# Products with the conditioning sums one turn later, and both context tiles behind the last token tile

## The chip, the cores and the metric

The kernel runs on one core of a Trainium2 chip. The metric is the device time of one execution in microseconds, the median of several runs.

## What is computed

One layer of a diffusion backbone over 1024 latent tokens of width 1024 and 256 context tokens. The part of the reference that matters here, cut:

```python
mod   = silu(c)     @ w_ada + b_ada          # 6 * 1024 numbers: shift, scale, gate, twice
mod_c = silu(c_ctx) @ w_ada + b_ada
h_lat = rms_norm(x, g_pre_mix)   * (1 + sc_m)  + sh_m
h_ctx = rms_norm(ctx, g_pre_mix) * (1 + csc_m) + csh_m
p_lat = h_lat @ w_in                         # 512 Fourier, 256 q, 128 kv, 32 rotary columns
p_ctx_kv = h_ctx @ w_in[:, KV_COL:]          # only kv and rotary columns
...
q = rms_norm(q_a, g_q_a) @ w_q_b             # later: attention, Fourier mixer, output projection
x = x + gt_m * rms_norm(y_lat, g_post_mix)
h2 = rms_norm(x, g_pre_ffn) * (1 + sc_f) + sh_f
x = x + gt_f * rms_norm(swiglu(h2), g_post_ffn)
```

All inputs are float32, and the result is wanted close to float32: every large product is made of three products of a "high" and a "low" half (`mm3`, or written out as in `back`).

## The kernel before

The kernel is cut into stages: the input projection (0 to about 150 us of the span), the Fourier mixer and the first query and key products, attention, the output projection, gate and up products of the channel mixer, and the down product. The change is in the second half of the input projection, `other_tiles` (from line 296), and at the start of `fourier`.

Eight token tiles of 128 rows (0 to 7) and two context tiles (c0, c1) are projected. Tiles 0 and 1 are done while `w_in` comes in (`first_tiles`). The other eight go through the loop of `other_tiles`, one turn each, in the order 2 to 7, c0, c1. For a tile there are these steps:

- `normed` (line 205): SyncE loads 128 rows to `xs`; ScalarE sums their squares (L86, `junk`); VectorE adds the epsilon (`var`), GpSimd takes the power (`rstd`) and scales the rows (L207).
- `transposed` (L212): TensorE turns the rows into a PSUM bank (`xT`).
- `front`: ScalarE applies shift and scale (L326, eight instructions, `h`), and makes the high half (`hh`, L50); VectorE makes the low half (`hl`, L56).
- `back` (L350): TensorE multiplies with `w_in`, 48 products for a token tile, 24 shorter ones for a context tile, into a bank `acc`.
- `after_project`: ScalarE copies the right columns of `acc` to `R` (L359, L362). For a token tile `fold` (L395 to L403) takes the Fourier columns on VectorE: tiles 0 to 3 are kept in `U`, with tiles 4 to 7 sums and differences are made (`eof`), which ScalarE and GpSimd split into halves (`Oh`, `Ol`, `EPh`, `EMh` and so on). Two buffers serve `eof`. Then `R` is normalized (GpSimd, L364 and L368) and its rotary columns are rotated (VectorE, `k1`, `k2`). The bank `acc` is free when the copy to `R` and the last reading by `fold` are done.
- `turn` (L382 to L388), a turn later: TensorE turns `R` into a bank `rps`, and ScalarE copies that to `q32`, `kv32`, `kr32`.

Beside this, two generators give out a few steps in each turn. `late_ada` makes three more parts of the conditioning: 24 blocks of `w_ada` of 512 KB are loaded into two buffers (`adraw`), and VectorE adds each, times its number, to a sum of 128 x 1024 (`adacc`, then `Gm`; L427, L429). After eight such sums a product with ones on TensorE (`gps`, L438 and L458) adds the partitions up; for the first two parts VectorE picks the diagonal (L440, `gdiag`) and reduces it (L442). `fourier_tables` loads the six slices of the transform's tables into two buffers (`traw`; L480); ScalarE makes their high halves (`toh`, `teh`) and GpSimd their low ones (`tol`, `tel`).

PSUM has eight banks of 2 KB a partition. `bankA` gives out three pieces of two banks in turn, to `xT`, `acc` and `gps`; `bankB` two pieces of one bank, to `rps`.

At the start of `fourier`, `attention_weights` loads the query, key and value weights; ScalarE scales them (`weight`, L588). The first transform (`positions(0)`, the products `po`, `pm`, `pp`) stands behind the last scaling of the query weights by `issue_after`, and then the rows of the last context tile are turned (`last_turn`), and the query products `qps` follow.

Each engine runs its instructions in order. The order is made when the program is built: the code's own order is the base, and a list scheduler of the framework moves instructions within an engine, so that a moved piece of code moves others too.

## Time and profile before

| | |
|---|---|
| median of 3 runs | 1269.03 us |
| lowest and highest run | 1265.46 and 1277.5 us |
| the profiled execution's own time | 1272.12 us |
| its span, first to last instruction | 1270.3 us |
| TensorE (PE) busy | 96% of the span |
| VectorE (DVE), ScalarE (ACT), GpSimd (POOL) busy | 69%, 50%, 40% |

The profile is one execution, read by an instruction timeline of each engine. A time in it is counted from the first instruction. A row that ends in brackets says how long the engine had stood idle before it and what the profile takes for the releaser; where that releaser had long been done, it was another one. POOL's spans are rough.

### The profile page before, as it was taken

What the parts mean: (1) busy time and instruction counts of PE and PEld (TensorE: products, weight loads), DVE (VectorE), ACT (ScalarE), POOL (GpSimd) and SP (SyncE); (2) the same over time, 40 slices, a digit from 0 to 9 for tenths busy, and PEclk for the clock granted to TensorE, in tenths of its full rate; (3) what the DMA queues carried; (4) which work ended last, traced back from release to release, by engine and by line L of the source; (5) the groups of instructions that cost most, each with busy time, mean ns of one, the idle gap of its engine ahead of it and who ended that gap; (6) DMA issues with size and microseconds to landing.
All of it is one profiled execution on the core that took longest, in us unless ns stands there. A gap on an engine that the chain in (4) does not pass through costs nothing.

```text
span 1270.3 us, 15471 instructions
## 1 busy us (share of the span) xinstructions
PE 1222.1 (96%) x5492; PEld 954.6 (75%) x5492; DVE 879.7 (69%) x1280; ACT 640.3 (50%) x1061; POOL 506.9 (40%) x332
## 2 busy tenths in 40 slices
PE   7999898999999998899999999999999999999997
PEld 5887676666666665678778888888888887887885
DVE  6777685555553546333778888777778775899697
ACT  6865657666767668265834444443344433222223
POOL 1275535777767770343183332233321300000083
PEclk8999989999999999899999999999999999999999
DMA  9576400000000015552025555342454368988645
GB/s 334 210 221 215 135 34 34 1 18 18 18 9 9 17 51 162 145 175 83 34 87 179 182 182 183 137 146 104 162 182 171 144 215 331 348 287 296 213 166 133
DMA packets 79573, 183.19 MB, mean 144 GB/s; under 512 B 9376, under 2 KB 41152, under 8 KB 79496
## 3 DMA queue, kind: packets, MB, share of 16 engines
q1 hardware_dynamic: 67832, 139.99, 33.2%
q10 hardware_dynamic: 11088, 40.11, 8.1%
q0 software_dynamic: 576, 2.10, 1.0%
q8 instruction: 44, 0.72, 0.2%
q14 instruction: 33, 0.27, 0.1%
HBM read 130.70 MB, written 51.45 MB: 143 GB/s over the span
## 4 chain that ended last, share of the span: by engine, by line
PE 52%; DMA 1%; ACT 1%; DVE 1%; issue 1%; POOL 1%; POOLq 0%; DVEq 0%; SPq 0%; ACTq 0%
PE gu L69 10%; PE gu L70 10%; PE gu L68 10%; PE dn L68 5%; PE dn L70 5%; PE dn L69 5%; PE y L798 5%; DMA unit<-zu 1%; DMA raw<-w_down 0%; POOL T L58 0%; PE T L212 0%; ACT H L326 0%; ACT unit L50 0%; DVE T6l L56 0%; DVE T7l L56 0%
## 5 line engine op out<-in xcount | busy, mean ns | idle before, releaser
L50 ACT ACTIVATE unit<-raw 128x512 fp32r<-128x512 f32 x171 | 105.2, 628 | 227.0 <-PE gu L70 101.6
L58 POOL TENSOR_TENSOR pl<-p,ph 128x1024 fp32r<-128x1024 f32 x70 | 168.3, 2409 | 65.4 <-ACT ph L50 41.8
L56 DVE TENSOR_TENSOR unit<-raw,unit 128x512 fp32r<-128x512 f32 x171 | 147.3, 869 | 28.0 <-ACT unit L50 27.7
L959 POOL TENSOR_TENSOR s<-raw 128x512 f32<-128x512 f32 x22 | 32.9, 1496 | 272.3 <-DMA raw<-w_gate 220.8
L740 DVE TENSOR_REDUCE mx<-sps 128x1 f32<-128x512 f32 (+1 forms) x192 | 104.2, 595 | 39.9 <-PE sps L739 39.9
L661 ACT ACTIVATE p<-S 128x1024 f32<-128x1024 f32 x80 | 81.5, 1023 | 74.0 <-PE S L658 67.0
L1179 POOL TENSOR_TENSOR rows<-rows,acc 128x512 f32<-128x512 f32 x8 | 13.4, 1704 | 213.1 <-DVE acc L1162 211.8
L50 ACT ACTIVATE ph<-p 128x1024 fp32r<-128x1024 f32 x80 | 84.2, 1058 | 2.0
L78 POOL TENSOR_TENSOR rstd<-var,mhalf 128x1 f32<-128x1 f32 x44 | 31.0, 705 | 111.6 <-DVE var L76 111.6
L69 PE MATMUL gu<-T,unit 128*128 128x512 f32 x176 | 69.4, 394 | 0.9 <-POOL T L58 0.9
L70 PE MATMUL gu<-Bh,unit 128*128 128x512 f32 x176 | 69.4, 394 | 0.5 <-DVE unit L56 0.5
L68 PE MATMUL gu<-Bh,unit 128*128 128x512 f32 x176 | 69.4, 394 | 0.0
L69 PE MATMUL gu<-Bl,unit 128*128 128x512 f32 x176 | 69.3, 394 | 0.0
L70 PE MATMUL gu<-T,unit 128*128 128x512 f32 x176 | 69.2, 393 | 0.0
L68 PE MATMUL gu<-T,unit 128*128 128x512 f32 x176 | 69.2, 393 | 0.0
L68 PE MATMUL dn<-unit 128*128 128x512 f32 x148 | 58.2, 393 | 0.6 <-ACT unit L50 0.6
L70 PE MATMUL dn<-unit 128*128 128x512 f32 x148 | 58.0, 392 | 0.0
L69 PE MATMUL dn<-unit 128*128 128x512 f32 x148 | 58.0, 392 | 0.0
L643 PE MATMUL O<-pl,Vh 128*65 128x512 f32 x160 | 53.8, 402 | 3.7 <-POOL pl L58 2.3
L798 PE MATMUL y<-woh,xth 128*128 128x512 f32 x128 | 52.3, 409 | 4.7 <-ACT xth L50 4.6
L350 PE MATMUL acc<-win,hh 128*128 128x512 f32 (+1 forms) x224 | 54.3, 361 | 1.3 <-DVE var L76 0.8
L1107 DVE TENSOR_TENSOR u<-u,gu 128x512 f32<-128x512 f32 x66 | 44.9, 683 | 15.3 <-PE gu L70 14.6
(423 smaller groups left out, 3489.5 us busy)
## 6 DMA issues: line engine op xcount, KB each, us to landing
zu<-zpair ACTq DMA_DIRECT2D x50, 512.0 KB
unit<-zu SPq DMA_DIRECT2D x47, 512.0 KB
adraw<-w_ada SPq DMA_DIRECT2D x32, 512.0 KB
units<-zu SPq DMA_DIRECT2D x27, 512.0 KB
zu<-zone ACTq DMA_DIRECT2D x24, 512.0 KB
raw<-w_gate SPq DMA_DIRECT2D x22, 512.0 KB
raw<-w_up SPq DMA_DIRECT2D x22, 512.0 KB
raw<-w_down SPq DMA_DIRECT2D x22, 512.0 KB
```

Source lines behind the costliest of these rows:

```text
L50: nc.scalar.activation(hi, src, AF.Copy)
L56: self.lastv = nc.vector.tensor_tensor(lo, src, hi.bitcast(F32), ALU.subtract)
L58: nc.gpsimd.tensor_tensor(lo, src, hi.bitcast(F32), ALU.subtract)
L68: self.nc.tensor.matmul(out, ah, bh, start=i == 0, stop=False)
L69: self.nc.tensor.matmul(out, ah, bl, start=False, stop=False)
L70: self.nc.tensor.matmul(out, al, bh, start=False, stop=i == n - 1)
L350: nc.tensor.matmul(acc[:, o], a[:, k, :], b[:, k, c], start=k == 0 and n == 0, stop=k == KT - 1 and n == 2)
L643: nc.tensor.matmul(O[0:m, ns], a, b[:, ns], start=k == 0 and i == 0, stop=k == NK - 1 and i == 2)
L661: nc.scalar.activation(p32, S, AF.Exp, scale=SCALE)
L740: self.lastmx = nc.vector.tensor_reduce(mx[:, i, c:c + 1], ps[:, 0:n], AX.X, ALU.max)
L798: nc.tensor.matmul(ps[:, ns], u[:, k, :], w[:, k, ns], start=k == 0 and i == 0, stop=k == KT - 1 and i == 2)
L1107: V(d, d, ps, ALU.add)
```

## The change

Four things change in the input projection, and one at the start of the Fourier mixer:

1. In a turn, the next tile's `front` comes before `late_ada`'s product, which was made at the end of the turn before; the sums are four in each of the first six turns (before: 4, 5, 5, 4 and so on). `gate` waits no turns before its product here (`rest=0`; the call in `down` keeps two). The diagonal is written back into the PSUM bank in place of `gdiag`.
2. Both context tiles are prepared early: the front of c0 before token tile 7's products, the front of c1 (with a third pair of buffers, which takes the place of `adacc` and `gdiag`) directly behind them. The rows of tile 7 are turned after the products of both context tiles.
3. A context tile's `acc` lies in a piece of `bankB`.
4. `fold` stands at the end of `after_project`.
5. `last_turn` stands under the same `issue_after` as `positions(0)`, so that the copies of its rows come behind the scaling of the query weights on ScalarE.

```diff
         late = self.late_ada()
-        nxt = self.front("x", self.psx)
+        fronts = deque([self.front("x", self.psx)])
...
-            if n + 1 < len(todo):
-                nxt = self.front(todo[n + 1][0], self.transposed(self.xs.pop(0), self.bankA("xT")))
+            def front(last=False):
+                fronts.append(self.front(todo[n + 1 + last][0], self.transposed(self.xs.pop(0), self.bankA("xT")), last))
+            if n + 2 < len(todo):
+                front()
+            if n in (2, 4, 6):
+                next(late)
             tail = self.back(src, i, *hs)
-            for f in pending:
-                f()
-            pending = [tail]
-            for _ in range(5 if n in (1, 2) else 4):
+            if n + 3 == len(todo):
+                front(True)
+            if src == "x" or i:
+                for f in pending:
+                    f()
+                pending = []
+            pending.append(tail)
+            for _ in range(4 if n < 6 else 0):
                 next(late, None)
...
-        hh = late.tile([P, KT, P], F32R, name="hh", bufs=2)
-        hl = late.tile([P, KT, P], F32R, name="hl", bufs=2)
+        hh = late.tile([P, KT, P], F32R, name="hh", tag="adacc", bufs=1) if last else late.tile([P, KT, P], F32R, name="hh", bufs=2)
+        hl = late.tile([P, KT, P], F32R, name="hl", tag="hl1", bufs=1) if last else late.tile([P, KT, P], F32R, name="hl", bufs=2)
...
-        acc = self.bankA("acc")
+        acc = self.bankA("acc") if lat else self.bankB("acc")
...
             nc.scalar.activation(R, acc[:, 512:928], AF.Copy)
-            self.fold(i, acc[:, 0:512])
...
             kr = k1
+            self.fold(i, acc[:, 0:512])
...
-        m = pool.tile([P, KT, P], F32, name="gdiag", bufs=1)
+        m = ps.rearrange("p (k c) -> p k c", c=P)
...
-    def gate(self, part, G, g, load, bank):
+    def gate(self, part, G, g, load, bank, rest=0):
         yield from self.ada_sums(part, G, load)
-        yield
-        yield
+        for _ in range(rest):
+            yield
...
             run(positions(0))
-        self.last_turn(bank)
+            self.last_turn(bank)
```

What this makes of the engines' orders is seen at three places.

TensorE, between tile 5's products and tile 6's (the second product with a sum; `rps` are tile 4's rows, `xT` is tile 7). Before:

```order
L350 MATMUL acc<-win_110,hl 128x416
L382 MATMUL rps<-ident,R 128x128 x2
L383 MATMUL rps<-ident,R 128x128
L384 MATMUL rps<-ident,k_1106 32x128
L438 MATMUL gps<-adacc,ones 128x512 x2
L212 MATMUL xT<-ident,xs 128x128 x8
L350 MATMUL acc<-win_110,hh 128x512
```

The change, at the same place:

```order
L361 MATMUL acc<-win_110,hl 128x416
L393 MATMUL rps<-ident,R 128x128 x2
L394 MATMUL rps<-ident,R 128x128
L395 MATMUL rps<-ident,k_1100 32x128
L212 MATMUL xT<-ident,xs 128x128 x8
L449 MATMUL gps<-adacc,ones 128x512 x2
L361 MATMUL acc<-win_110,hh 128x512
```

The eight transposes have gone ahead of the product; nothing else moved there.

ScalarE, around the copy of tile 3's `acc` to `R` (`traw` are table slices: the first two of these rows are slices 2 and 3 of the odd table, `teh` is from the even one). Before:

```order
L50 ACTIVATE toh_852<-traw_1137 128x512
L50 ACTIVATE toh_852<-traw_1278 128x512
L359 ACTIVATE R_941<-acc_892 128x416
L50 ACTIVATE teh_854<-traw_1422 128x516
L86 ACTIVATE junk_944,ss_945<-R_941 128x128
```

The change:

```order
L50 ACTIVATE toh_852<-traw_1133 128x512
L50 ACTIVATE toh_852<-traw_1269 128x512
L50 ACTIVATE teh_854<-traw_1420 128x516
L370 ACTIVATE R_941<-acc_892 128x416
L397 ACTIVATE q32T_104<-rps_966 128x2x128
```

The first half-table of the even transform now stands ahead of the copy that frees tile 3's bank. On GpSimd, `tol` of slice 2 (the reader that frees the buffer for this even slice) has gone behind the scaling of tile 6's rows.

ScalarE, from the copy of tile 7's `acc` on (`rps_1544` and `rps_1566` are tile 6's rows; `h` is context tile c1). Before:

```order
L359 ACTIVATE R_1507<-acc_1458 128x416
L386 ACTIVATE q32T_104<-rps_1544 128x2x128
L86 ACTIVATE junk_1522,ss_1523<-R_1507 128x128
L86 ACTIVATE junk_1530,ss_1531<-R_1507 128x256
L50 ACTIVATE Oh_846<-eof_1509 128x512
L387 ACTIVATE kv32T_105<-rps_1544 128x128
L388 ACTIVATE kr32T_106<-rps_1544 32x128
L326 ACTIVATE h_1577<-xT_1568,SH_97,A_96 128x128 x2
L50 ACTIVATE EPh_848<-eof_1514 128x512
L50 ACTIVATE EMh_850<-eof_1518 128x512
L326 ACTIVATE h_1577<-xT_1568,SH_97,A_96 128x128 x3
```

The change:

```order
L370 ACTIVATE R_1505<-acc_1456 128x416
...
L50 ACTIVATE Oh_846<-eof_1529 128x512
L336 ACTIVATE h_1551<-xT_1542,SH_97,A_96 128x128 x3
L50 ACTIVATE EPh_848<-eof_1534 128x512
L50 ACTIVATE hh_1552<-h_1551 128x512
L50 ACTIVATE EMh_850<-eof_1538 128x512
L336 ACTIVATE h_1551<-xT_1542,SH_97,A_96 128x128 x4
L397 ACTIVATE q32T_104<-rps_1566 128x2x128
L50 ACTIVATE hh_1552<-h_1551 128x512
L398 ACTIVATE kv32T_105<-rps_1566 128x128
L399 ACTIVATE kr32T_106<-rps_1566 32x128
```

The three copies of tile 6's rows, which stood around `Oh`, have gone behind `EMh` and the rest of c1's `h`.

## Rows read from the trace of the kernel before

**Rows 1.** The page: busy time, share of the span, instructions.
```profile
PE 1222.1 (96%) x5492; PEld 954.6 (75%) x5492; DVE 879.7 (69%) x1280; ACT 640.3 (50%) x1061; POOL 506.9 (40%) x332
```
**Rows 2.** TensorE's timeline: start, length, instruction, idle time before it and its releaser.
```profile
84.42 1.98 PE L438 MATMUL gps<-adacc,ones 128*128 128x512 f32 x4 [2.09 <-DVE var L76]
...
87.03 1.08 PE L350 MATMUL acc<-win,hh 128*128 128x512 f32 x4
...
111.44 1.98 PE L438 MATMUL gps<-adacc,ones 128*128 128x512 f32 x4 [2.36 <-DVE adacc L429]
...
115.06 1.08 PE L350 MATMUL acc<-win,hh 128*128 128x512 f32 x4 [0.76 <-DVE var L76]
...
136.51 0.38 PE L382 MATMUL rps<-ident,R 128*128 128x128 f32 x2
...
143.24 0.44 PE L382 MATMUL rps<-ident,R 128*128 128x128 f32 x2 [2.37 <-POOL R L368]
...
146.15 0.50 PE L350 MATMUL acc<-win,hh 128*128 128x256 f32 x2 [0.54 <-ACT h L326]
...
150.12 0.33 PE L383 MATMUL rps<-ident,R 128*128 128x128 f32 x1 [0.63 <-POOL R L364]
...
156.81 0.50 PE L68 MATMUL qps<-qTh,wqh 128*128 128x512 f32 x1 [1.83 <-ACT wqh L588]
```
**Rows 3.** ScalarE's timeline: tile 6's rows arrive, tile 3's copy, the even table.
```profile
77.53 1.06 ACT L86 ACTIVATE junk<-xs 128x1024 bf16<-128x1024 f32 x1 [0.78 <-DMA xs<-x]
...
84.21 0.50 ACT L359 ACTIVATE R<-acc 128x416 f32<-128x416 f32 x1
86.44 0.63 ACT L50 ACTIVATE teh<-traw 128x516 fp32r<-128x516 f32 x1 [1.74 <-DMA traw<-dft_e]
...
89.23 0.64 ACT L50 ACTIVATE teh<-traw 128x516 fp32r<-128x516 f32 x1 [0.75 <-DMA traw<-dft_e]
```
**Rows 4.** GpSimd by tile: durations in ns, minimum, median, maximum.
```profile
L58 POOL TENSOR_TENSOR tol<-traw,toh x4: 1271/1986/2263, 67.4 to 84.4; 128x512 fp32r<-128x512 f32 x4
L207 POOL TENSOR_SCALAR xs<-xs,rstd x6: 1118/1158/2531, 66.4 to 124.2; 128x1024 f32<-128x1024 f32 x6
L58 POOL TENSOR_TENSOR Ol<-eof,Oh x4: 1257/1796/2307, 103.8 to 140.8; 128x512 fp32r<-128x512 f32 x4
```
**Rows 5.** SyncE's queue: issue of the two even slices.
```profile
82.10 0.33 SPq L480 DMA_DIRECT2D traw<-dft_e  x1
...
85.67 0.33 SPq L480 DMA_DIRECT2D traw<-dft_e  x1
```
**Rows 6.** ScalarE's timeline from tile 2's copy to the next `h`.
```profile
70.54 0.52 ACT L359 ACTIVATE R<-acc 128x416 f32<-128x416 f32 x1 [2.78 <-POOL tol L58]
...
73.33 1.86 ACT L326 ACTIVATE h<-xT,SH,A 128x128 f32<-128x128 f32 x5
```
**Rows 7.** VectorE's timeline: the diagonal, the ninth sum, the seventeenth, tile 5's fold.
```profile
88.67 1.21 DVE L440 TENSOR_TENSOR gdiag<-gps,ident 128x1024 f32<-128x1024 f32 x1
89.80 0.74 DVE L427 TENSOR_SCALAR adacc<-adraw,cols 128x1024 f32<-128x1024 f32 x1
...
112.70 0.87 DVE L427 TENSOR_SCALAR Gm<-adraw,cols 128x1024 f32<-128x1024 f32 x1 [1.31 <-DMA adraw<-w_ada]
...
114.24 0.67 DVE L403 TENSOR_TENSOR U<-U,acc 128x512 f32<-128x512 f32 x1
```
**Rows 8.** ScalarE's timeline: the last split of tile 7's fold, the query weights.
```profile
142.86 0.63 ACT L50 ACTIVATE EMh<-eof 128x512 fp32r<-128x512 f32 x1 [1.25 <-DVE eof L400]
...
151.48 2.01 ACT L50 ACTIVATE qTh<-q32T 128x1024 fp32r<-128x1024 f32 x2
...
155.60 2.19 ACT L588 ACTIVATE wqh<-wqraw,cols 128x1024 fp32r<-128x1024 f32 x2
```
**Rows 9.** Busy time of each engine in two stretches, then TensorE's granted clock, DMA share, GB/s.
```profile
158.70:162.10 3.40, 3.37 (x9) 2.09 (x8) 3.40 (x6) 2.37 (x4) 0.00 (x0) 0.50 0.00 0
...
140.00:150.00 10.00, 6.59 (x40) 4.70 (x38) 5.87 (x11) 6.85 (x20) 7.31 (x8) 1.00 0.43 143
```

More of the change, by code (lines that the diff above doesn't have):

```diff
@@ L300, in other_tiles @@
         late = self.late_ada()
-        nxt = self.front("x", self.psx)
+        fronts = deque([self.front("x", self.psx)])
         pending = [self.after_project(i, self.accs[i]) for i in range(2)]
         for n, (src, i) in enumerate(todo):
-            hs = nxt
+            hs = fronts.popleft()
             if n + 2 < len(todo):
@@ L321, in other_tiles @@
             pass
-        self.last_turn = pending[0]
+        self.last_turn, = pending
     def modulate(self, outs, ps, scale, shift):
@@ L326, in modulate, with front @@
             self.lastm = self.nc.scalar.activation(out, ps[:, k * P:(k + 1) * P], AF.Identity, bias=shift[:, k:k + 1], scale=scale[:, k:k + 1])
-    def front(self, src, ps):
+    def front(self, src, ps, last=False):
         late = self.late
@@ L1145, in down @@
         bank = lambda name: self.psD.tile([P, D], F32, name=name, tag="D", bufs=4)
-        gate = self.gate(5, self.Gf, t["g_post_ffn"], lambda: p2.tile([P, D], F32, name="adraw", tag="adraw", bufs=1), lambda name: bank(name)[:, 0:512])
+        gate = self.gate(5, self.Gf, t["g_post_ffn"], lambda: p2.tile([P, D], F32, name="adraw", tag="adraw", bufs=1), lambda name: bank(name)[:, 0:512], 2)
         def product(i, group, dst, first):
```

## The prediction

> **What bounds the kernel now.** I read the page first: TensorE is busy 96% of the span [rows 1], so time is to be won or lost only where TensorE stands idle, or where its clock is low. Then I read TensorE's timeline through the changed stretch, from tile 4 to the first query product. Seven waits stand there [rows 2]: 2.09 and 2.36 us before the two `gps` products, 0.76 before tile 6's products, 2.37 before tile 7's rows are turned, 0.54 before c1's products, 0.63 before c0's rows, and 1.83 before the first query product. Their sum is 10.58 us, 0.8% of the run, and this is all that the change can win there. About 1% is also what a measurement of this kernel can tell from no change. Last I read the other engines at these places, because each wait is the end of a chain on ScalarE, VectorE, GpSimd or a load, and the change moves instructions on all of them. The reader is to see, in each of the groups below, not how long an instruction is, but what stands in front of it on its engine.
>
> I walk along the time axis of the profiled execution and ask, for four places of TensorE, when they come after the change: tile 4's products (87.03 before), tile 6's products (115.06), the first transform (right behind 150.12) and the first query product (156.81) [rows 2].
>
> **Place 1, tile 4's products: 2.4 us later.** Here the change means to win: the transposes, 0.8 us, go ahead of the product, into its wait of 2.09. But tile 4's `acc` takes the piece of PSUM that tile 3 used, and that is free only when ScalarE has copied it to `R` and VectorE has copied it to `U`. Before, the copy to `R` ran at 84.21, ahead of the first even table slice, which waited for its load until 86.44 [rows 3]. Now that slice (`teh`) stands ahead of the copy, and everything hangs on its load. The load needs the buffer that GpSimd frees with `tol` of slice 2, and that `tol` now stands behind the scaling of tile 6's rows. The chain, from rows:
>
> - Tile 6's rows arrive at 77.5 [rows 3] (its load is issued behind one more table load, so up to 0.6 later: 77.5 to 78.1). The sum of squares, `var` and `rstd` take about 2.0 (1.06 of them the row shown), the scaling 1.1 to 2.5, `tol` 1.3 to 2.3 [rows 4]. The buffer is free between 81.9 and 84.7.
> - From the issue of an even slice to its use went 86.44 - 82.10 = 4.3 and 89.23 - 85.67 = 3.6 us [rows 3, 5]. So `teh` starts at a time T between 85.5 and 89.0; I take the middle, T = 87.1.
> - `teh` 0.55, `R` 0.5, `k1` and `k2` 0.55, `U` 0.7: the bank is free at T + 2.3 = 89.4, against 87.03. The product with the sum (ready before 86) is hidden in this wait, so it is no gain at all.
>
> **Place 2, tile 6's products: 4.6 us later in all.** Between the two places lie 24 us of products, but the sums pace this stretch: the ninth starts at 89.80 and the seventeenth at 112.70 [rows 7], and in between each load can be issued only when the sum two places before it has freed its buffer. VectorE waited for such loads again and again, the last time 1.31 us. If the ninth sum is late, all are. After the change the ninth stands behind the first half of tile 5's `hl` and behind the reduction. ScalarE takes 2.8 us from `R` to the first `h`, of which 0.85 were a second tile's rows that are not there now, 1.75 for five `h` [rows 6] and 0.65 for `hh`, a split of the same size as `teh` [rows 3]. With T = 87.1: `R` at T + 0.55, `hh` done at T + 4.9, `hl` at T + 5.5, the reduction 1.15, the ninth sum at T + 6.65 = 93.75. That is 3.95 later than before, and the seventeenth comes at 116.65. From there tile 5's fold has to free tile 6's bank: before, from 112.70 to 114.24 + 0.67, 2.2 us; now `k1` and `k2` stand ahead of the fold, so about 2.85. Tile 6's products start at 116.65 + 2.85 + 0.15 = 119.65, against 115.06. With T at its ends the difference is 2.8 to 6.3. The second product waits for the sixteenth sum inside the same time and costs nothing more; its transposes in front win nothing.
>
> The diagonal written to PSUM: the multiplication took 1.21 us [rows 7]. No row shows VectorE writing so wide to PSUM; I bound it by half and by twice as long (0.6 to 2.4) and take 1.21. It lies between `U` and `hl`, where VectorE waits for `hh` about 1 us; only above 2.2 us would it reach the path. The longer hold of the bank ends tens of matmuls before its next user.
>
> **Place 3, the first transform: 0.4 us later relative to the end of tile 7's products.** From there (136.51) to the end of c0's rows before the transform it took 13.8 us [rows 2]. Tile 7 itself has no new wait. What goes: 2.37 for tile 7's rows, which are now turned last, and 0.63. What comes instead: c1's `acc` takes the piece of `bankB` in which tile 6's rows lay, and the three copies out of it now stand on ScalarE behind `EMh` and c1's `h`. `EMh` waits for VectorE's `eof`, which waits for GpSimd's `Ol` to free a buffer, as before: 142.86 is 6.35 after 136.51 [rows 8, 2]. Now both scalings of `R` stand ahead of `Ol` (0.65 for a second `rstd` and about 0.5 for the scaling, against `Ol` of 1.3 to 2.3 [rows 4]): `EMh` at 6.9 to 7.3. Then 0.55 for it, four `h` 1.5, three copies and one `hh` 1.35: c1 can start 10.2 us after tile 7's end (9.5 to 10.9). TensorE has xT, rows, the third product and c0 to do in this time, 5.9 us, so it stands idle for more than 4. Then c1 2.85, tile 7's rows 0.43, about 0.5 for the copy that frees c1's bank, c0's rows 0.2: 14.2 against 13.8, so +0.4 (-0.5 to +1.2).
>
> **Place 4, the first query product: 1.5 us won.** Before, the scaling of the query weights started at 155.60, behind the copies of c1's rows, and TensorE waited 1.83 [rows 8, 2]. Now it follows `qTh` (2.0 us) at once; `qTh` can start about 1 us after the first transform's start, so the first half of the weights is there after 4.1 us, while the transform and the last rows take 4.5. The wait goes. VectorE's low halves come no earlier against the products, which cost about 0.3 again. I take -1.5 (-2.0 to -0.9).
>
> **The sum.** +4.6 + 0.4 - 1.5 = +3.5 us on the profiled execution: 1272.1 becomes 1275.6. That execution stands 3.1 above the median of the runs, 1269.0, from which the same 3.5 gives the forecast: 1272.5 us. With all ends: 2.8 - 0.5 - 2.0 = +0.3 and 6.3 + 1.2 - 0.9 = +6.6. All behind the query products is bound by TensorE and moves along; loads there get more time, not less. The lower clock is kept as it was, with one stretch more or less as its price: the clock was 0.50 for 3.4 us after the wait at 156.81 [rows 9], 1.2 instead of 2.4 GHz, and cost 1.7. So the forecast's own range is 1266 to 1279, with the scatter of the runs.
>
> The Trainium skill (TensorE: Matmul & The Clock Gate, "The HAM clock gate") says that the clock is low by default and that an idle TensorE is put back to it until it has been active again. The trace agrees at 158.70, but not always: from 140 to 150, with the wait at 143.24, it was 1.00 throughout [rows 9]. By that rule the idle time of over 4 us before c1's products would bring one more such fall, and the sum would be +5.2.
>
> **The rivals.**
>
> - The change works as meant: every sum and row is ready, and the waits go except about 0.6. That is 10.0 us, 1259 us. For it speaks that all waits shown end on results that the change asks for later. Against it: two of the new waits end on freed PSUM, not on results. Chance 0.12.
> - The load of the even slice is early: `tol` of slice 2 runs before T matters, tile 3's copy is not held up, and tile 4 comes at about 86.2. Then the ninth sum is 0.5 late, tile 6 about 1.2, and with places 3 and 4 the sum is +0.1: 1269 us. For it: `tol` takes only 1.3 us where nothing disturbs it [rows 4], and an even load 3.6 [rows 3, 5]. Against it: the order puts `tol` behind rows that arrive at 77.5. Chance 0.15.
> - The clock falls in the long wait before c1 and stays low through c1's products, the rows and into the transform: three stretches of 3.4 us at half clock, 5.1 us, on the upper end of the sums, 6.6: 1281 us, slower by about 1%. It decides from the point where TensorE's idle time before c1 is above 4 us. For it: rows 9 and an idle time longer than any in this stretch before. Against it: TensorE is busy right before. Chance 0.13.
>
> The forecast keeps 0.60.
>
> **How the numbers follow.** Faster by over 1% is below 1256.3: a third of the first rival, 0.04. Slower by over 1% is above 1281.7: half of the last rival and a little of the forecast's tail, 0.10. Within 1%: 0.86. The range holds the forecast's own, and reaches to most of the first and the last rival: 1259 to 1283.
>
> **What would show it.** Right: tile 4's products start near 89 on a wait that ends with `U` or `R`, ScalarE idle before `teh` with tile 3's `R` behind it; tile 6's near 119 to 120; an idle time of 4 to 5 us before c1's products that ends with ScalarE's copies of rows; no wait before the first query product. Wrong: `teh` before 85, or the ninth sum before 91, which would take away the largest term; or c1 starting less than 9 us after tile 7's end.

## The result and the profile after

| | before | after |
|---|---|---|
| median of the runs | 1268.8 us (14 runs) | 1277.94 us (14 runs) |
| lowest and highest | 1265.46, 1277.5 | 1276.42, 1280.18 |
| the profiled execution's own time, span | 1272.12, 1270.3 | 1277.23, 1275.1 |

The ratio is 1.0065 (95% interval 1.0051 to 1.0078): 8.2 us slower on 1268.8, within 1%. The two profiled executions stand only 5.1 us apart.

TensorE's timeline of the changed kernel, where [rows 2] stood for the one before:

```profile
84.08 1.96 PE L449 MATMUL gps<-adacc,ones 128*128 128x512 f32 x4 [1.04 <-DVE adacc L440]
90.75 1.89 PE L361 MATMUL acc<-win,hh 128*128 128x512 f32 x4 [4.72 <-DVE var L76]
...
115.77 1.88 PE L449 MATMUL gps<-adacc,ones 128*128 128x512 f32 x4
118.98 1.08 PE L361 MATMUL acc<-win,hh 128*128 128x512 f32 x4 [1.32 <-DVE U L414]
...
140.42 1.03 PE L212 MATMUL xT<-ident,xs 128*128 128x128 f32 x8
143.02 1.95 PE L469 MATMUL gps<-Gm,ones 128*128 128x512 f32 x4 [1.13 <-DVE Gm L440]
153.04 0.80 PE L361 MATMUL acc<-win,hh 128*128 128x256 f32 x2 [5.24 <-ACT kr32T L399]
158.83 0.30 PE L394 MATMUL rps<-ident,R 128*128 128x128 f32 x1 [0.44 <-ACT R L372]
159.00 0.48 PE L68 MATMUL po<-toh,Oh 128*128 128x512 f32 x1
163.41 0.50 PE L68 MATMUL qps<-qTh,wqh 128*128 128x512 f32 x1
```

The waits before the products with sums have shrunk or gone, and so have those for tile 7's rows and before the first query product (163.41 has no bracket). In their place stand 4.72 us before tile 4's products and 5.24 before c1's, which wait for the last copy of tile 6's rows (152.72, below); elsewhere stand 1.04 before the first product with a sum, 1.32 before tile 6's products (0.76 before), 1.13 before the third product with a sum and 0.44 before c0's rows. At 90.75 the bracket names `var`, which had nothing to do with it; of what frees tile 3's bank, VectorE's copy to `U` was last (it ended at 90.61).

ScalarE, in place of [rows 3] and [rows 8]:

```profile
78.59 1.06 ACT L86 ACTIVATE junk<-xs 128x1024 bf16<-128x1024 f32 x1 [2.01 <-DMA xs<-x]
...
87.81 0.63 ACT L50 ACTIVATE teh<-traw 128x516 fp32r<-128x516 f32 x1 [6.50 <-DMA traw<-dft_e]
88.34 0.50 ACT L370 ACTIVATE R<-acc 128x416 f32<-128x416 f32 x1
...
141.14 0.50 ACT L370 ACTIVATE R<-acc 128x416 f32<-128x416 f32 x1
...
149.72 0.63 ACT L50 ACTIVATE EMh<-eof 128x512 fp32r<-128x512 f32 x1 [2.57 <-DVE eof L411]
...
152.72 0.27 ACT L399 ACTIVATE kr32T<-rps 32x128 f32<-32x128 f32 x1
```

GpSimd and VectorE, in place of [rows 4] and [rows 7]:

```profile
82.83 3.45 POOL L58 TENSOR_TENSOR tol<-traw,toh 128x512 fp32r<-128x512 f32 x2
...
146.63 1.28 POOL L58 TENSOR_TENSOR Ol<-eof,Oh 128x512 fp32r<-128x512 f32 x1
147.88 1.26 POOL L58 TENSOR_TENSOR EPl<-eof,EPh 128x512 fp32r<-128x512 f32 x1
```

```profile
90.75 1.22 DVE L451 TENSOR_TENSOR gps<-gps,ident 128x1024 f32<-128x1024 f32 x1
94.47 0.74 DVE L438 TENSOR_SCALAR adacc<-adraw,cols 128x1024 f32<-128x1024 f32 x1
...
116.39 0.75 DVE L438 TENSOR_SCALAR Gm<-adraw,cols 128x1024 f32<-128x1024 f32 x1 [1.30 <-DMA adraw<-w_ada]
...
147.95 1.74 DVE L411 TENSOR_TENSOR eof<-U 128x512 f32<-128x512 f32 x1 [1.99 <-POOL Ol L58]
```

SyncE could issue the first even slice's load only at 85.08, against 82.10 in [rows 5]. Two stretches by windows (columns as in [rows 9]) show the clock at its lower level, 1.2 GHz, behind both long waits:

```profile
90.00:94.00 4.00, 3.25 (x9) 2.82 (x10) 3.31 (x8) 3.99 (x11) 1.93 (x4) 0.50 0.55 210
...
153.00:157.00 4.00, 3.96 (x18) 3.96 (x19) 1.05 (x3) 0.71 (x3) 0.93 (x2) 0.50 0.60 173
```

From the first transform on the loss no longer grows. The transform starts 8.7 us later than before, the first query product 6.6, the end of the span 4.8 (8.2, 6.1 and 4.0 against a second profile of the kernel before, which comes next).

### The profile page after: what moved, and what is told of

The parts are those of the page before. It is cut to its first block, busy times and chain, and to the rows that moved or that the text cites. A ratio compares the mean times of both kernels' runs of the same rounds, so it can differ in the third digit from the quotient of the medians.

```text
span 1275.1 us, 15489 instructions
## 1 busy us (share of the span) xinstructions
PE 1223.9 (96%) x5492; PEld 955.7 (75%) x5492; DVE 879.7 (69%) x1280; ACT 640.3 (50%) x1061; POOL 506.3 (40%) x332
## 4 chain that ended last, share of the span: by engine, by line
PE 52%; DMA 1%; ACT 1%; DVE 1%; issue 1%; POOL 1%; POOLq 0%; DVEq 0%; SPq 0%; ACTq 0%
PE gu L69 10%; PE gu L70 10%; PE gu L68 10%; PE dn L68 5%; PE dn L70 5%; PE dn L69 5%; PE y L809 5%; DMA unit<-zu 1%; DMA raw<-w_down 1%; POOL T L58 0%; PE T L212 0%; ACT H L336 0%; ACT unit L50 0%; DVE T6l L56 0%; DVE T7l L56 0%
## 5 line engine op out<-in xcount | busy, mean ns | idle before, releaser
L361 PE MATMUL acc<-win,hh 128*128 128x512 f32 (+1 forms) x224 | 57.9, 378 | 11.3 <-ACT kr32T L399 5.2
L361 PEld LDWEIGHTS acc<-win,hh 128*128 128x128 f32 x224 | 43.3, 202 | 17.8 <-ACT junk L86 5.5
```

Source lines behind the costliest of these rows:

```text
L361: nc.tensor.matmul(acc[:, o], a[:, k, :], b[:, k, c], start=k == 0 and n == 0, stop=k == KT - 1 and n == 2)
```

## The experiments

The theory behind the forecast (theory 1) is that the loss sits in banks which are freed late, because the order of the other engines has changed. Its first rival (theory 2) is that the sums, four a turn and with their product a turn later, set the pace. The table has the places that the runs are read by, in us of each profiled execution; "tile 7's end" is the start of the instruction behind its products. Each profile is one execution, and some stand well off the median of their runs: that of the kernel before, a second time, 5.2 us above it, that with the fold back for tile 7 alone 5.8 below, that of the first two products alone 4.3 below.

| kernel | ratio to before, 95% interval | tile 4 | tile 6 | tile 7's end | transform | query |
|---|---|---|---|---|---|---|
| before | | 87.03 | 115.06 | 136.51 | 150.32 | 156.81 |
| before, again | 0.9987 (0.9968 to 1.0006) | 85.88 | 112.84 | 134.28 | 150.82 | 157.29 |
| the change | 1.0065 (1.0051 to 1.0078) | 90.75 | 118.98 | 140.42 | 159.00 | 163.41 |
| fold alone | 1.0061 (1.0042 to 1.0080) | 90.44 | 116.85 | 138.29 | 156.85 | 163.33 |
| change, fold put back | 1.0030 (1.0015 to 1.0046) | 88.00 | 115.12 | 138.12 | 155.01 | 159.41 |
| change, even slice pinned | 1.0063 (1.0043 to 1.0083) | 87.25 | 116.37 | 137.81 | 157.70 | 162.12 |
| change, fold back for tile 7 | 1.0056 (1.0035 to 1.0076) | 89.57 | 118.37 | 139.81 | 156.87 | 161.27 |
| products alone | 1.0039 (1.0021 to 1.0057) | 85.52 | 116.23 | 139.70 | 155.50 | 161.99 |
| first two products alone | 1.0021 (1.0006 to 1.0035) | 85.78 | 114.49 | 137.51 | 151.30 | 157.77 |
| contexts alone | 1.0007 (0.9995 to 1.0019) | 87.85 | 114.49 | 135.94 | 153.27 | 159.74 |
| change, c1 in another bank | 1.0056 (1.0038 to 1.0074) | 90.31 | 119.15 | 142.48 | 158.18 | 163.19 |
| fold put back, c1 in another bank | 1.0023 (1.0005 to 1.0041) | 86.64 | 116.55 | 138.00 | 156.40 | 161.41 |
| weights alone | 0.9987 (0.9971 to 1.0003) | 87.56 | 114.54 | 135.99 | 150.02 | 154.42 |
| change, TensorE kept busy | 1.0068 (1.0050 to 1.0085) | 91.83 | 123.45 | 144.88 | 161.43 | 165.84 |

**Before, a second time.** No edit.

> The kernel before, unchanged, for a second profile of it: its first one lies 3 us above its median, that of the changed kernel 0.7 below its own. Theory 1: the same waits within 0.4 us at the same places (tile 4's products 24 to 24.5 us behind the transposes for tile 5's predecessor as before, 2.1 and 2.4 us before the two products with sums), and what differs between executions is the number of stretches at clock 0.5 behind them: this one has fewer or as many in 140 to 200 than the first (three slices below 0.9 there). Rival: the places themselves move by 2 us or more from execution to execution, so that one profile of each kernel can't be compared to a microsecond.

```profile
109.20 1.99 PE L438 MATMUL gps<-adacc,ones 128*128 128x512 f32 x4 [1.27 <-DVE adacc L429]
...
112.84 1.08 PE L350 MATMUL acc<-win,hh 128*128 128x512 f32 x4 [0.78 <-DVE var L76]
...
142.49 0.44 PE L382 MATMUL rps<-ident,R 128*128 128x128 f32 x2 [2.37 <-POOL R L368]
...
142.98 3.58 PE L458 MATMUL gps<-Gm,ones 128*128 128x512 f32 x4
```

The rival holds: the waits before the two products with sums are 1.66 and 1.27 us instead of 2.1 and 2.4, and tile 6 comes 2.2 us earlier than in the first profile, as the loads behind the sums happen to land. The transform comes 0.5 later. From tile 7's end to the transform this execution took 16.54 us, the first 13.81: c0's products waited 1.26 us for a low half, and behind the wait of 2.37, where the clock was 1.00 in the first profile, it was 0.50 from 143 to 146, so that the third product took 3.58 us instead of 1.88. Over 140 to 200 the clock was a little higher all the same (0.91, 1.00 and 0.91 in the thirds; in the first profile 0.97, 0.86 and 0.91). So single rows at tile 6, and the way from tile 7's end to the transform, are read to 2 or 3 us; times are judged by the ratios.

**Fold alone**, on the kernel before:

```diff
             nc.scalar.activation(R, acc[:, 512:928], AF.Copy)
-            self.fold(i, acc[:, 0:512])
...
             kr = k1
+            self.fold(i, acc[:, 0:512])
```

> The kernel before with one part of the change alone: fold at the end of after_project. The program's order then has the first even slice ahead of tile 3's copy and tol of slice 2 behind the scaling of tile 6's rows, as in the changed kernel; products with sums, context tiles and query weights are as before. Theory 1: tile 4's products start 3 to 4.5 us later than before (87.03), at 90 to 91.5, with a wait of over 2 us between the product and them, and the time is 1272 to 1275 (before 1269). Theory 2 (late sums): no change, 1267.5 to 1270.5.

```profile
87.49 0.63 ACT L50 ACTIVATE teh<-traw 128x516 fp32r<-128x516 f32 x1 [6.36 <-DMA traw<-dft_e]
88.03 0.50 ACT L359 ACTIVATE R<-acc 128x416 f32<-128x416 f32 x1
```

```profile
145.50 3.10 PE L458 MATMUL gps<-Gm,ones 128*128 128x512 f32 x4
...
150.92 0.80 PE L350 MATMUL acc<-win,hh 128*128 128x256 f32 x2 [2.33 <-ACT h L326]
```

```profile
140.00:160.00 20.00, 15.32 (x72) 11.80 (x71) 10.76 (x20) 11.64 (x34) 10.83 (x13) 0.74 0.45 138
```

Theory 1's place is there (tile 4 at 90.44), with the same wait of `teh` ahead of the copy as in the changed kernel, and theory 2 can't give this, since products and sums were untouched. But the loss is 7.7 us (0.0061 of 1269), more than the 3 to 6 expected: the transform is late by 6.5 (6.0 against the second profile of before), tile 6 only by 1.8 (4.0). A second effect sits behind tile 7. From its end to the transform it took 4.75 us more than in the first profile of before, and the waits are only 1.1 of that (2.11, 2.33 and 0.23 against 2.37, 0.54 and 0.63): the clock was 0.50 from 146 to 156, and TensorE was at work longer.

**Fold put back** in the changed kernel:

```diff
             nc.scalar.activation(R, acc[:, 512:928], AF.Copy)
+            self.fold(i, acc[:, 0:512])
...
             kr = k1
-            self.fold(i, acc[:, 0:512])
```

> The change with one part undone: fold stands right behind the copy to R again, ahead of the norms and the rotation. With that the program's order has tile 3's copy to R ahead of the first even table slice again, and GpSimd's tol of slice 2 ahead of the scaling of tile 6's rows. Theory 1 (holds): the loss sits in two PSUM pieces that are freed late, tile 3's by that order and tile 6's rows' by ScalarE's order; so tile 4's products start at 86 to 87.5 on the trace's clock (changed kernel: 90.75), tile 6's at 115 to 116.5 (118.98), no stretch at clock 0.5 follows tile 4's wait, and the time is 1278 less 3.5 to 5.5: 1272.5 to 1274.5. Theory 2 (late sums): the four sums a turn and the product a turn later set the pace, whatever fold does; tile 6's products then still start at 118 to 119, and the time stays at 1277 to 1279.

```profile
85.24 3.42 PE L449 MATMUL gps<-adacc,ones 128*128 128x512 f32 x4 [2.74 <-ACT R L370]
...
88.00 1.50 PE L361 MATMUL acc<-win,hh 128*128 128x512 f32 x4
...
115.12 1.56 PE L361 MATMUL acc<-win,hh 128*128 128x512 f32 x4 [2.07 <-DVE var L76]
...
149.14 0.79 PE L361 MATMUL acc<-win,hh 128*128 128x256 f32 x2 [4.81 <-ACT kr32T L399]
```

The time falls by 4.4 us (1.0065 to 1.0030), in the range of theory 1, and tile 6 is back. Two details missed: tile 4 starts 0.5 later than expected, and the clock falls all the same, behind a wait of 2.74 us (the product takes 3.42 us where 1.96 is usual).

**Even slice pinned**: fold stays last, but `teh` is kept behind tile 3's copy.

```diff
-            nc.scalar.activation(R, acc[:, 512:928], AF.Copy)
+            self.copies[i] = nc.scalar.activation(R, acc[:, 512:928], AF.Copy)
...
-                self.split(hi[:, s, :], lo[:, s, :], raw[:, 0:w], "a", "p")
+                with (self.tc.issue_after(self.copies[3].ins) if src is t["dft_e"] and s == 0 else nullcontext()): self.split(hi[:, s, :], lo[:, s, :], raw[:, 0:w], "a", "p")
```

> The change with fold left at the end, but the first even slice's split (teh) pinned on ScalarE behind tile 3's copy to R; GpSimd's tol of slice 2 stays behind the scaling of tile 6's rows, so the load of that slice stays as late as in the changed kernel (teh near 87.8). Theory 1: the copy runs at 84 to 84.5, tile 4's products start at 86 to 87 in spite of the late load, and the clock does not fall there; tile 6's start at 115.5 to 117; time 1273 to 1275. If the late load itself is what counts (it still holds ScalarE's h for tile 5 up to about 89.5), tile 4 starts early, but tile 5 or tile 6 waits in its place and the time stays above 1276. Theory 2 (late sums): 1277 to 1279.

```profile
87.25 1.08 PE L361 MATMUL acc<-win,hh 128*128 128x512 f32 x4 [1.06 <-DVE U L406]
...
150.87 0.79 PE L361 MATMUL acc<-win,hh 128*128 128x256 f32 x2 [6.25 <-ACT kr32T L399]
```

Tile 4 (0.25 us later than expected) and tile 6 do what theory 1 says, and yet the time stays above 1276 (1277.25), though neither tile 5 nor tile 6 waits in tile 4's place. The 3.5 us won at tile 4 are 1.3 at the transform: c1's products wait 6.25 instead of 5.24, and the clock was 0.50 from 147 to 157. The chain behind tile 7's fold is a floor of its own.

**Fold back for tile 7 alone**:

```diff
             nc.scalar.activation(R, acc[:, 512:928], AF.Copy)
+            if i == 7: self.fold(i, acc[:, 0:512])
...
-            self.fold(i, acc[:, 0:512])
+            if not (i == 7): self.fold(i, acc[:, 0:512])
```

> The changed kernel with fold put back behind the copy for tile 7 alone. On GpSimd, Ol then stands between the two scalings of R and no longer behind both, and the splits of tile 7's fold come earlier; nothing before tile 7's copy moves. Tile 4 and tile 6 as in the changed kernel (90.75, 118.98). Theory: EMh comes 6.9 to 7.7 us after tile 7's end instead of 9.3, c1's products 10.2 to 11 after it instead of 12.6, and the time is 1.3 to 2.5 us below the changed kernel: 1275.4 to 1276.6. Rival: GpSimd's Ol is not what holds EMh there (two late sums on VectorE are), c1 moves by less than 0.7, and the time stays within 0.7 of 1277.9.

```profile
145.43 1.29 POOL L58 TENSOR_TENSOR Ol<-eof,Oh 128x512 fp32r<-128x512 f32 x1
146.69 1.01 POOL L379 TENSOR_SCALAR R<-R,rstd 128x256 f32<-128x256 f32 x1
```

```profile
146.75 0.69 DVE L412 TENSOR_TENSOR eof<-U 128x512 f32<-128x512 f32 x1 [1.71 <-POOL Ol L58]
```

`Ol` now runs between the scalings, the third `eof` takes 0.69 us again, and `EMh` comes at 147.47, 7.7 us after tile 7's end instead of 9.3, as expected; c1's products 11.5 instead of 12.6, a little less than expected. The place moves as the theory says. The time (1277.15 median, 1.0056) does not tell it from the changed kernel: the intervals overlap, and the profiled execution is the fastest of its six.

**Products alone**, on the kernel before: the product behind the next `front`, four sums a turn, `rest=0`.

```diff
+            if n in (2, 4, 6): next(late)
             tail = self.back(src, i, *hs)
...
-            for _ in range(5 if n in (1, 2) else 4):
+            for _ in range(4 if n < 6 else 0):
```

> The kernel before with the first part of the change alone: the product with the sums a turn later behind the transposes, four sums a turn, no rest before the third product; fold, context tiles, banks and weights as before (the diagonal goes to gdiag). Here the program's order keeps tile 3's copy ahead of the first even slice and tol of slice 2 ahead of the scaling of tile 6's rows. Theory 1: no new hold; tile 4's products 0 to 1 us earlier than before (87.03), tile 6's -1.5 to +0.5 (115.06); time 0.5 to 1.5 us below before. Theory 2 (late sums): the products and sums are late and tile 6's products start at 117 or later; time 2 us or more above before.

```profile
112.43 2.39 PE L439 MATMUL gps<-adacc,ones 128*128 128x512 f32 x4 [3.67 <-DVE var L76]
...
116.23 1.89 PE L351 MATMUL acc<-win,hh 128*128 128x512 f32 x4 [1.41 <-DVE var L76]
```

Here theory 1 fails by itself: without any of its holds the kernel is 4.9 us slower (0.0039). Tile 4 is 1.5 us early, but the second product gives that back: it waits 3.67 us for the sixteenth sum, and the clock falls behind it: from tile 6's products to tile 7's end it took 23.5 us, in both profiles of before 21.4. The time is the one that theory 2 expected; the place is not quite, since tile 6 comes at 116.23 and not at 117 or later.

**The third product back** at its old place, behind tile 7's rows; no other engine's order moves.

```diff
-            if n in (2, 4, 6): next(late)
+            if n in (2, 4): next(late)
...
-            for _ in range(4 if n < 6 else 0):
+            for _ in range(4 if n != 6 else 6):
```

> The run with the products moved alone (1275.2, tile 6 at 116.23, transform 15.8 us behind tile 7's end), with the third product back at its old place, behind tile 7's rows; every other engine's order is the same as in that run. If the third product ahead of c0 is what costs, the transform comes 13.8 to 14.5 us behind tile 7's end and the time is 1271 to 1273. If the first two cost (the load of c0's rows then stands one load earlier in SyncE's queue, beside the load of the 14th sum), tile 6 still starts 1 us or more behind the kernel before, and the time stays at 1274 to 1276.5.

```profile
114.49 1.07 PE L351 MATMUL acc<-win,hh 128*128 128x512 f32 x4 [2.21 <-DVE var L76]
```

The transform is 13.8 us behind tile 7's end, as in the first profile of before (the second has 16.5), and 2.3 of the 4.9 us go (0.0021 against 0.0039, intervals that overlap). So the third product, ahead of c0, may cost about as much as the first two; clear of the noise this is not shown. What the first two cost is settled in part: behind the wait of 2.21 us the clock was 0.50 from 116 to 119, and from tile 6's products to tile 7's end it took 23.0 us instead of 21.4. Tile 6 itself stands within the 2 us by which it scatters.

**Contexts alone**: the second and third part on the kernel before, with the diagonal in the bank (whose multiplication took 1.22 us in the changed kernel, 1.21 in [rows 7]).

```diff
-            for f in pending:
-                f()
-            pending = [tail]
+            if n + 3 == len(todo):
+                front(True)
+            if src == "x" or i:
+                for f in pending:
+                    f()
+                pending = []
+            pending.append(tail)
...
-        acc = self.bankA("acc")
+        acc = self.bankA("acc") if lat else self.bankB("acc")
```

> The kernel before with the second and third part of the change alone: both context tiles' fronts behind the last token tile's, tile 7's rows turned behind c1's products, context acc in bankB (and the diagonal in the bank, since the third pair of buffers takes gdiag's room); products with sums, fold and weights as before. Theory 1: the wait of 2.37 for tile 7's rows goes, but c1 is held by ScalarE's copies of tile 6's rows behind EMh, so that the first transform comes 13.4 to 15 us after tile 7's end as against 13.8, and the time is within 1.2 us of before. Rival (the part works as meant): the transform comes 11 to 12.5 us after tile 7's end and the time is 1.5 to 3 us below before.

```profile
147.60 0.50 PE L361 MATMUL acc<-win,hh 128*128 128x256 f32 x2 [4.60 <-ACT kr32T L399]
```

No gain and no loss that can be measured (1.0007). The wait of 2.37 us for tile 7's rows has become one of 4.60 before c1, held by the copies of tile 6's rows. The transform comes 17.3 us after tile 7's end, more than the 13.4 to 15 expected; the clock averaged 0.65 from 147 to 151, through c1's products.

**c1 in another bank** (of the changed kernel; every order stays).

```diff
-        acc = self.bankA("acc") if lat else self.bankB("acc")
+        acc = self.bankB("acc") if not lat and i == 0 else self.bankA("acc")
```

> The change with context tile c1's products in a piece of bankA (that of tile 7) and not in the piece of bankB in which tile 6's rows lay; every engine's order of instructions is the same. Theory 1: c1's first 12 products follow c0's at once, near 147.6, and only the second half waits, for hh and hl of c1 behind EMh, to 152.5 to 153.3; the first transform starts 2.5 to 4 us earlier relative to tile 7's end than in the changed kernel (18.6), so 14.6 to 16.1, and the time is 1274 to 1275.5. Rival: c1's own h and hh, behind EMh on ScalarE, would hold it as long, and the time stays within 1 us of 1278.

```profile
153.36 0.39 PE L361 MATMUL acc<-win,hl 128*128 128x256 f32 x1 [4.22 <-DVE hl L56]
```

c1 starts at 148.74, at once behind c0, and then stands 4.22 us at its first low half, which VectorE makes behind the late fold. The transform is 15.7 us after tile 7's end instead of 18.6, as expected. The time, 1275.92, is just above the range; by the ratios (1.0056 against 1.0065, intervals that overlap) it is not told from the changed kernel. The bank was one of two things that held c1.

**Fold put back and c1 in another bank**, both edits together.

> The change with fold put back behind the copy and, beside that, c1's products in a piece of bankA. Theory 1: tile 4 as in the run with fold put back; then c1's first 12 products follow c0's at once, and the second half waits only for hl, so that the first transform starts 2 to 3 us earlier than in that run (155.0): 152 to 153; time 1270.4 to 1272 (fold put back: 1273.35). Rival: as in the changed kernel, where the other bank gained 2.0 in all, or less, because the wait for c1's own hl takes the place of the bank: 1272.5 to 1273.5.

```profile
112.74 1.95 PE L449 MATMUL gps<-adacc,ones 128*128 128x512 f32 x4 [2.87 <-DVE var L76]
...
148.57 0.54 PE L361 MATMUL acc<-win,hh 128*128 128x256 f32 x2 [2.59 <-ACT hh L50]
...
151.00 0.58 PE L361 MATMUL acc<-win,hl 128*128 128x256 f32 x1 [1.88 <-DVE hl L56]
```

The rival is the nearer one: 1273.17 against 1273.35 (by the ratios, 1.0023 and 1.0030, the two are not told apart), and the transform comes at 156.40, not at 152 to 153. With the bank free, c1 waits for its own halves.

**Weights alone**, on the kernel before.

```diff
-        self.last_turn(bank)
+            self.last_turn(bank)
```

> The kernel before with the last part of the change alone: last_turn under the same issue_after as the first transform, so that ScalarE copies c1's rows behind the scaling of the query weights. Theory 1: the wait of 1.83 before the first query product goes, and with it the stretch at clock 0.5 behind it: first query product 4.4 to 4.8 us behind the transform's start (before: 6.5), keys 8.8 to 10.2 (before 11.7); time 1.5 to 2.5 us below before. Rival: VectorE's low halves of the weights come no earlier and the products wait for them instead: within 0.7 us of before.

The wait of 1.83 is gone: 4.4 us from the transform to the query products (6.5 before), 8.7 to the keys (11.7; in the second profile of before 10.5). The time, 0.9987 (0.9971 to 1.0003), is on the side expected, but the second run of the unchanged kernel gave the same ratio; a gain of 1.7 us is not shown.

**TensorE kept busy** in the two long waits of the changed kernel.

```diff
-        for n in range(2):
+        for n in [0, 1] * (3 if part == 4 else 1):
...
-        for n in range(2):
+        for n in [0, 1] * (1 if rest else 3):
```

The first and the third product with sums are made three times over.

> The changed kernel with TensorE kept at work in its two longest waits: the first product with sums (before tile 4) and the third (before c0) are each made three times over into the same bank, 3.9 us more work at each; no result changes. If what the waits cost is partly the clock, then tile 4's products still start at 90.3 to 91.2 (they wait for the copies that free the bank), but take 10.1 us instead of 12.4, and c1's, with a wait of 1 to 2.5 us instead of 5.2, take 2.9 instead of 4.75. Tile 6's products still start at 118 to 119.5, since the sums set their time, so the first gain is given back; the second stays: 1275.5 to 1276.8 against 1277.9. If the clock falls all the same, or its price is hidden, 1277.3 to 1279.

Tile 4's products and c1's by windows:

```profile
91.80:101.90 10.10, 10.07 (x48) 9.06 (x49) 6.59 (x11) 5.04 (x12) 5.30 (x7) 1.00 0.21 74
157.30:161.20 3.90, 3.53 (x28) 3.24 (x28) 2.12 (x4) 1.06 (x5) 0.93 (x2) 1.00 0.89 261
```

```profile
95.90 1.22 DVE L451 TENSOR_TENSOR gps<-gps,ident 128x1024 f32<-128x1024 f32 x1
...
99.43 0.74 DVE L438 TENSOR_SCALAR adacc<-adraw,cols 128x1024 f32<-128x1024 f32 x1
```

With TensorE at work the clock stays up, and tile 4's products take 10.1 us instead of 12.4, c1's about 2.9 instead of 4.75. But tile 4 starts 0.6 us later than expected, and the diagonal now stands on VectorE behind the first half of `hl`: it ran at 95.90 instead of 90.75, the ninth sum started at 99.43 instead of 94.47, and tile 6 fell back to 123.45. Price and gain cancel (1277.67): the clock's price is shown at the two places, not in the whole.

## Why the prediction was right, and where it was off

The forecast was 1272.5 us, within 1%, by a loss of 3.5; the result lies in the upper part of the range, at the end of the forecast's own (1266 to 1279). The measured loss, 8.2 us by the ratio, is over twice the forecast's: the width of the range (1259 to 1283) holds it, not the sum. Along the time axis, with the profile of the changed kernel against the two of the kernel before:

| | forecast | measured | against the second profile |
|---|---|---|---|
| tile 4's products | +2.4 | +3.7 | +4.9 |
| tile 6's products, tile 7's end | +4.6 | +3.9, +3.9 | +6.1, +6.1 |
| transform, relative to tile 7's end | +0.4 | +4.8 | +2.0 |
| first query product, relative to the transform | -1.5 | -2.1 | -2.1 |
| the rest | 0 | -1.8 | -2.1 |
| sum | +3.5 | +4.8 of span | +4.0 of span |

That the sum along the profile comes near is partly luck: the 4.4 us that were missing at the transform meet 3.1 that the other steps had too much. How the loss divides between tile 6 and the transform depends on the execution that stands for the kernel before; both together do not: 8.7 and 8.2 us at the transform, where the forecast had 5.0.

**Place 1 was right in its mechanism.** `teh` started at 87.81 where T was put at 87.1, for the reason given: tile 6's rows were summed at 78.59, `tol` of slice 2 ran from 82.83, and the load went out at 85.08. That T came out so near is luck: from the rows' sum to their scaling it took 3.15 us instead of 2.0, so that the buffer came free at 85.0, behind the forecast's 81.9 to 84.7, and the slice was used 2.7 us behind its issue, where 3.6 to 4.3 were allowed. (By the forecast's own terms the upper end is 84.9, and the middle of 85.5 and 89.0 is 87.25, not 87.1.) The bank was free 2.8 us later (2.3 forecast; `k1` alone took 0.96 beside GpSimd). Fold alone shows what the forecast did not say: the move of `fold` by itself reorders ScalarE and GpSimd there, far from the moved lines. Not counted was the clock: 0.50 from 90 to 95.5, so that tile 4's products took 12.4 us, against 10.1 with TensorE kept busy. In this profile that cost nothing at tile 6, where the fold stood behind the seventeenth sum, which had waited 1.30 us for its load.

**Place 2 was right in its size.** The ninth sum came at 94.47 (forecast 93.75), the seventeenth at 116.39 (116.65), tile 6 at 118.98 (119.65). The loads caught up 1.0 us in between. Against the second profile the loss is 6.1, near the upper end of the forecast's 2.8 to 6.3 (its own terms, with T at its ends, give 3.0 to 6.5).

**Place 3 is the step that failed: the term of +0.4 measured +4.8** (+2.0 against the second profile of before). The forecast had c1 start 10.2 us after tile 7's end, though its terms add up to 10.5; it started after 12.6. From tile 7's end to its copy 0.5 us were lost; from the copy to `EMh` it took 149.72 - 141.14 = 8.6 us against 6.1 before (136.76 to [rows 8]; 6.9 in the second profile), where the forecast had allowed for 0.55 to 0.95 more; from `EMh` to c1 nothing changed (3.3 in both); and from c1 to the transform it took 6.0 instead of 4.2 (4.0 in the forecast). Of the 2.5 us before `EMh`, 1.4 are `Ol`, which runs 5.5 us after the copy instead of 4.1 (both scalings ahead of it, and a later first `eof`), and 1.05 are the third `eof`: 1.74 us long beside GpSimd's `EPl`, where in the kernel before it ran alone:

```profile
142.13 0.69 DVE L400 TENSOR_TENSOR eof<-U 128x512 f32<-128x512 f32 x1 [1.42 <-POOL Ol L58]
```

That fold's place does this the runs show: from the copy to `EMh` it took 7.8 to 8.6 us in five kernels with fold last and 5.9 to 7.4 in eight with fold early, the one with tile 7's alone put back among them (7.1); the third `eof` took 1.73 to 1.76 us in the five and 0.69 to 0.96 in the eight. The Trainium skill (SBUF — State Buffer, "SBUF: two separate sides") says that a VectorE instruction with two inputs in SBUF contends with a GpSimd instruction that reads SBUF, because the second input comes through a read interface that both share. The trace agrees: `EPl` started 0.07 us ahead and ended at 149.14, and the `eof` was done 0.55 later, a little less than the 0.69 that it takes alone. No sentence of the forecast had weighed this. Fold's place is not all of place 3: contexts alone, with fold early, have 17.3 us from tile 7's end to the transform.

**The clock, +1.8 us of place 3, was a rival's point.** The wait before c1 was 5.2 us, and the clock fell to 0.50 behind it; c1's products took 4.75 us instead of the 2.85 of the forecast (2.9 with TensorE kept busy). The Trainium skill (TensorE: Matmul & The Clock Gate, "The HAM clock gate") gave one fall more than the forecast for this wait, and the trace agrees here. The clock was low for 6.8 us, 4.1 of them with TensorE at work, not for the three stretches of 3.4 on which the third rival's 1281 rested. But low clocks of that length do occur there: about 10 us with fold alone and with the even slice pinned.

**Place 4 was right**: the wait went, -2.1. Not counted was that the stretch of lower clock behind it [rows 9] went too: from query product to keys 4.4 us instead of 5.2. The second profile of the kernel before did not have that stretch either (4.0 us). The last 1.0 us of the -1.8 lies behind the keys and is within what two executions differ by.

**What is left.** The sum along the profiles is 4.8 to 5.1, the medians say 9.1 and the ratio 8.2. The forecast carried its sum from the profiled execution to the median as it was; both profiled executions had the same mean clock (0.986 and 0.987), while over the timed runs it was on average 0.984 with the change and 0.988 to 0.990 before. So for the timed runs the forecast's "The lower clock is kept as it was" does not hold. An estimate from these means: 0.004 to 0.006 of 1275 us are 10 to 15 us more at 0.50, which cost 5 to 8 us where TensorE is at work all the time. Which stage they lie in is not shown.

**The parts.** Alone they measure +7.7 (fold), +4.9 (products), +0.9 (contexts) and -1.7 (weights), 11.8 us together; the change has 8.2. With intervals of 1.5 to 2.4 us either way on each part the two sums can't be told apart. That parts can overlap the pinned slice shows: most of what is won at tile 4 is lost again before c1. The rival that all works as meant fell with the first two. No run is shown to be faster than the kernel before.

## What to carry to other kernels

Where a scheduler orders the instructions, read its order on every engine after moving even one call: `fold`, moved behind a few small instructions, put a waiting table slice ahead of a copy that frees a bank. A wait taken away from TensorE is only won if the next result is ready too; here all but the one before the query products ended at a bank, a load or a half that came no earlier. Take a second profile of the unchanged kernel before a place is read to a microsecond. And test the parts alone: two of four cost more than the forecast gave to the whole change.

## What the hardware showed

A VectorE add of 128 x 512 with both operands in SBUF took 0.69 us alone and 1.74 beside a GpSimd instruction that read SBUF. The clock fell to 0.50 behind waits of 2.74, 4.72 and 5.24 us, but the length of a wait did not decide it alone. Behind the wait of 2.37 before tile 7's rows it stayed at 1.00 in the first profile of the kernel before [rows 2, 9] and was 0.50 from 143 in the second; behind the wait of 1.83 before the query products it was 0.50 from 158.7 in the first and stayed at 1.00 in the second; and behind one of 2.87 (fold put back and c1 in another bank, at 112.74) it stayed at 1.00. In one kernel, tile 6 came 2.2 us earlier in the second of two executions, and the next stage 0.5 later.
